# One 4 KB PSUM tile for both halves of a score group, and value products over two query tiles

## The chip, the cores and the metric

The kernel runs on one NeuronCore of a Trainium2 chip. Its engines are TensorE (PE in the profile, with its weight loads as PEld), VectorE (DVE), ScalarE (ACT), GpSimd (POOL) and SyncE (SP), which issues the DMAs. The metric is the device time of one execution in microseconds. Three runs of the kernel before took 1154.95, 1155.72 and 1156.66 us; the median is 1155.72 us.

## The reference

Two layers of a transformer work on 256 context and 256 latent tokens of width 1024. A layer modulates its input, projects it, and has three groups of attention heads side by side: A, six heads of differential attention (two softmax maps of 32-wide queries and keys per head, the second taken off the first with a learned weight); B, six heads with a neighbourhood window and a bias; C, four heads with compressed queries and keys, 96 wide. Then come an output projection, a norm, a gated ConvFFN and a norm. Context tokens read context alone, latent tokens read both; the second layer computes latent queries only.

```python
def _diff_attend(q, k, v, lam, scale):
    s = jnp.einsum('bhqcd,bhkcd->bhcqk', q, k).astype(jnp.float32) * scale
    p = jax.nn.softmax(s, axis=-1)
    p = p[:, :, 0] - lam * p[:, :, 1]
    return jnp.einsum('bhqk,bhkd->bhqd', p.astype(v.dtype), v)

def _softmax_attend(q, k, v, scale):
    s = jnp.einsum('bhqd,bhkd->bhqk', q, k).astype(jnp.float32) * scale
    p = jax.nn.softmax(s, axis=-1)
    return jnp.einsum('bhqk,bhkd->bhqd', p.astype(v.dtype), v)
```

## The kernel before

Weights are split into a high and a low part (`whi` by ACT at L121, `wlo` by DVE at L122), and each product is three matmuls (`mm3`, L134 to L136). The projections for heads A, B and C and the attention units that use them are traced in an order given by the string `ORDERS` (one unit is two heads); a scheduler then sets each engine's own order from that trace, and every engine works through its order strictly.

An attention unit goes over the streams "lat" (512 keys) and, in the first layer, "ctx" (256 keys), and in each over two query tiles of 128 rows. For each query tile `sco` makes **a score group**: two score maps, one per PSUM bank (`sc`, two tiles of 512 floats). For A these are the two maps of one head, for B the two heads of the unit; both have three matmuls per map (`score3`, L626), and the two maps lie in different row groups of the PE array (32 rows each for A, 64 for B). C has one matmul per head (L831). So there are 24 + 12 lat groups and 12 + 6 ctx groups of A and B, and 12 pairs of C.

`softmax_rows` does, for each map, a row maximum (DVE, L381), the exponential with its row sum (ACT, L384) and a reciprocal (DVE, L385). A then multiplies the second reciprocal with the learned weight (L701), scales the second map (L702) and joins the two (L703); B and C scale each map (L674), and B first adds its bias to the map in PSUM (L745). The probabilities are transposed on PE (L392) and copied by ACT (L393) into `pT`, and the value products (`pv`, L400) run once per query tile with 128 columns for each of the two heads, which lie in the two column halves of the array. `drain` keeps transposes and value products one step behind the scores.

PSUM has three banks `acc`, one `ada`, two `sc` and two `tp`. The `sc` banks also serve early projections (`evb`), a value projection (`proj_vk`) and, between the layers, `early`.

Of the kernel before, what the change touches and what calls it, by code (L numbers as in the profile page):

```python
# [77 lines left out]
def build(nc, tc, st, I, out):  # L78
# [18 lines left out]
    def acc():  # L97
        return bank("acc", 3)
# [2 lines left out]
        return bank("ada", 1)  # L101

    def scp():
        return bank("sc", 2)

    def tpp():
        return bank("tp", 2)
# [277 lines left out]
        V.reciprocal(sums[:, 1:2], sums[:, 0:1])  # L385
        return p, sums

    def to_pT(ap, p, nk):
        pT = ap.tile([P, 4, 128], F32, tag="pT", name="pT", bufs=4)
        pt = tpp()  # L390
        for kc in range(nk // P):
            T.transpose(pt[:, 128 * kc:128 * kc + 128], p[:, 128 * kc:128 * kc + 128], ident)  # L392
        S.copy(pT[:, 0:nk // P, :], pt[:, 0:nk].rearrange("p (k q) -> p k q", q=P))  # L393
        return pT

    def pv(po, qt, pTs, vt, c0, nk):
        n = nk // P
        for kc in range(n):
            for e in range(2):
                T.matmul(po[64 * e:64 * e + 64, 128 * qt:128 * qt + 128],  # L400
                         lhsT=vt[:, kc, c0 + 64 * e:c0 + 64 * e + 64],
                         rhs=pTs[e][:, kc, :], start=(kc == 0), stop=(kc == n - 1), tile_position=(0, 64 * e))

# [86 lines left out]
    nxt = load_round(1)  # L490
    ada_round(0, raws)
    ef = [acc() for _ in EF]
    evb = {pr: scp() for pr in (1, 0)}
    for s in range(4):
        ks = (2 * s, 2 * s + 1)
        w = split_early(wes[s])
# [39 lines left out]
    for l in range(L):  # L536
# [60 lines left out]

        def proj_vk():
            w = vkw
            for t in (2, 3, 0, 1):  # L600
                tok = slice(128 * t, 128 * t + 128)
                po = acc() if last and t % 2 else scp()
                for k in range(KD):
                    hi, lo = w[k // 3 * 3]
                    mm3(po[:, 0:288], hT["hi"][:, k, tok], hT["lo"][:, k, tok], hi[:, k % 3, :], lo[:, k % 3, :],
                        k == 0, k == KD - 1)
                pump(PF)
                S.copy(vt[:, t, 256:544], po[:, 0:288])
# [31 lines left out]

        def heads(i, sco, vv, c0, fin):
            for name, q0, nk in streams:
                box = {}
                for qt in range(2):
                    qs = slice(q0 - q0c + 128 * qt, q0 - q0c + 128 * qt + 128)
                    pTs = []

                    def finish(qt=qt, pTs=pTs, box=box, nk=nk, q0=q0):
                        if qt == 0:
                            box["po"] = tpp()  # L650
                        pv(box["po"], qt, pTs, vv, c0 + 128 * i, nk)
                        if qt == 1:
                            fin(box["po"][:, 0:256], slice(q0 - q0c, q0 - q0c + 256))

                    for e in range(2):
                        p = sco(2 * i + e, e, qs, qt, nk, name)

                        def transposed(p=p, e=e, pTs=pTs, nk=nk, finish=finish):
                            pTs.append(to_pT(ap, p, nk))
                            if e == 1:  # L660
                                late[1].append(finish)

                        late[0].append(transposed)
                        drain(0, 1)
                        drain(1, 1)
# [29 lines left out]

        def attn_a(i):
            def sco(h, e, qs, qt, nk, name):
                banks = [scp() for _ in range(2)]
                score3(banks, aqs[i], aks[i], 32, 64 * e, qs, nk)
                (p0, s0), (p1, s1) = [softmax_rows(sc, nk, ap, f"p{m}") for m, sc in enumerate(banks)]  # L700
                V.tensor_tensor(s1[:, 1:2], s1[:, 1:2], lam[:, 2:3], ALU.mult)  # L701
                V.tensor_scalar_mul(p1[:, 0:nk], p1[:, 0:nk], s1[:, 1:2])  # L702
                V.scalar_tensor_tensor(p0[:, 0:nk], p0[:, 0:nk], s0[:, 1:2], p1[:, 0:nk], ALU.mult, ALU.add)  # L703
                return p0

            def fin(po, c):
                sq = ap.tile([P, 256], F32, tag="sq", name="sq", bufs=2)
                S.activation(sq, po, AF.Square)
                pm = tpp()
                T.matmul(pm[:, 0:256], lhsT=K["bones"], rhs=sq, start=True, stop=True)  # L710
# [19 lines left out]
        def attn_b(i):  # L730
            banks = []

            def sco(h, e, qs, qt, nk, name):
                if e == 0:
                    banks[:] = [scp() for _ in range(2)]
# [12 lines left out]
            heads(i, sco, vt, 416 if i else 384, simple_fin(3 + i))  # L748
# [77 lines left out]
                S.copy(mq[h // 2][64:96, h % 2, :], q[32 * h:32 * h + 32, qc])  # L826

        def attn_c(i):
            def sco(h, e, qs, qt, nk, name):
                sc = scp()  # L830
                T.matmul(sc[:, 0:nk], lhsT=mq[i][0:96, e, qs], rhs=mk[i][0:96, e, 0:nk], start=True, stop=True)  # L831
                return normed(sc, nk)

            heads(i, sco, vm, 0, simple_fin(6 + i))

# [10 lines left out]
                not done and kk == 0, len(done) == 3 and kk == 1)  # L846

        def out_early(jb):
            for hf in range(2 if last else 1):
                w = wsplit(I["w_out"][l, hf, jb], 1024)  # L850
                for t in toks:
# [305 lines left out]
        def tail2(ts):  # L1157
# [5 lines left out]
            if 2 in ts:  # L1163
                flush()
                new_h()
            else:
                for i in (12, 13, 14):
                    w = kview(wsplit(I["w_f"][l + 1, i], 1024), KD)
                    early[i] = (acc() if i < 14 else scp(), w, [(CTX, LO + HI)] if i == 14 else [])
                    f_mm(early[i][0], w, 0, LO + HI, LAT, True, i < 14)  # L1170
                w = {kb: kview(wsplit(I["w_v"][l + 1, 0, kb], 1024), 4) for kb in range(2)}
                early["v"] = ({1: scp(), 0: acc()}, w, LO + HI, (0,))
# [107 lines left out]
```

## Time and profile before

| | us |
|---|---|
| median of three runs | 1155.72 |
| profiled execution | 1158.58 |
| its span | 1156.5 |
| PE busy | 1107.0 (96%) |
| DVE busy | 836.1 (72%) |
| ACT busy | 591.2 (51%) |

The span holds the instructions; about 2 us lie around it. Matmuls are pipelined, so the time that one takes is the distance to the start of the next, not its own duration. Attention lies at 118 to 309 us in the first layer and at 785 to 927 us in the second; between and behind them PE works through the FFN without a gap.

### The profile page before, as it was taken

To read this page: it belongs to the slowest core of one execution; us is meant where nothing else is said; L and a number is where in the kernel's file an instruction comes from. 1 tells how busy PE (TensorE), PEld (TensorE's weight loads), DVE (VectorE), ACT (ScalarE), POOL (GpSimd) and SP (SyncE) were. 2 spreads that over 40 slices of the span, in tenths; PEclk is the share of its full clock that TensorE was granted. 3 is DMA by queue.
4 is the path that set the end of the run, shared out by engine and by line. 5 is a ranking of instruction groups with operands and counts; after the bars stand their busy time and mean duration, and the time that the engine had idled before them with its cause. 6 is when DMAs were issued, how large, how long until landed. Compare 5 with 4: busy or idle time off the path is not lost.

```text
span 1156.5 us, 17907 instructions
## 1 busy us (share of the span) xinstructions
PE 1107.0 (96%) x6776; PEld 902.1 (78%) x6776; DVE 836.1 (72%) x1505; ACT 591.2 (51%) x1063; POOL 83.8 (7%) x104
## 2 busy tenths in 40 slices
PE   5999999999998999999999999999999979999997
PEld 3877666686778888887888877897778758999985
DVE  4544677757588887986977687666766777888755
ACT  4345556656548644444352245555555656666541
POOL 0000100003123000000000002110000420000000
PEclk9999999999999999999999999998999988999999
DMA  9767112112143554643558894533111333555662
GB/s 362 295 241 279 58 37 74 37 37 86 51 164 97 197 169 144 199 152 116 186 174 309 311 328 131 176 94 99 53 55 56 128 132 121 183 183 188 201 203 89
DMA packets 58213, 179.19 MB, mean 155 GB/s; under 512 B 7024, under 2 KB 12432, under 8 KB 58128
## 3 DMA queue, kind: packets, MB, share of 16 engines
q1 hardware_dynamic: 58128, 178.05, 45.8%
q8 instruction: 54, 0.88, 0.3%
q14 instruction: 31, 0.25, 0.1%
HBM read 176.94 MB, written 1.08 MB: 154 GB/s over the span
## 4 chain that ended last, share of the span: by engine, by line
PE 85%; DVE 6%; ACT 2%; issue 2%; POOL 2%; DMA 2%; SPq 0%; DVEq 0%; POOLq 0%; ACTq 0%
PE acc L134 21%; PE acc L135 21%; PE acc L136 21%; PE sc L626 6%; PE tp L392 3%; PE tp L400 3%; PE sc L831 2%; DVE wlo L122 1%; PE sc L134 1%; PE sc L135 1%; PE sc L136 1%; POOL xn L344 1%; DMA rawr<-in_w_ada_e 1%; PE ada L234 1%; PE ada L136 1%
## 5 line engine op out<-in xcount | busy, mean ns | idle before, releaser
L121 ACT CAST whi<-raw 128x1024 fp32r<-128x1024 f32 (+3 forms) x204 | 212.0, 1043 | 248.7 <-PE acc L135 124.4
L122 DVE TENSOR_TENSOR wlo<-raw,whi 128x1024 fp32r<-128x1024 f32 (+3 forms) x204 | 248.4, 1221 | 121.4 <-ACT whi L121 117.1
L134 PE MATMUL acc<-hhi,whi 128*128 128x256 f32 (+1 forms) x960 | 327.3, 341 | 3.5 <-ACT hhi L360 3.5
L135 PE MATMUL acc<-hlo,whi 128*128 128x256 f32 (+1 forms) x960 | 325.4, 339 | 0.5 <-DVE hlo L361 0.3
L136 PE MATMUL acc<-hhi,wlo 128*128 128x256 f32 (+1 forms) x960 | 324.1, 338 | 0.4 <-DVE wlo L122 0.4
L134 PEld LDWEIGHTS acc<-hhi,whi 128*128 128x128 f32 x960 | 184.7, 193 | 28.2 <-issue 5.4
L135 PEld LDWEIGHTS acc<-hlo,whi 128*128 128x128 f32 x960 | 184.9, 193 | 22.2 <-issue 3.6
L136 PEld LDWEIGHTS acc<-hhi,wlo 128*128 128x128 f32 x960 | 184.6, 192 | 22.1 <-issue 3.8
L384 ACT ACTIVATE p<-sc,nm 128x512 f32<-128x512 f32 (+1 forms) x132 | 81.4, 619 | 26.0 <-DVE nm L381 24.5
L381 DVE TENSOR_REDUCE nm<-sc 128x1 f32<-128x512 f32 (+1 forms) x132 | 77.3, 598 | 22.7 <-PE sc L626 15.9
L393 ACT COPY pT<-tp 128x512 f32<-128x512 f32 (+1 forms) x96 | 49.4, 516 | 56.2 <-PE tp L392 55.8
L626 PE MATMUL sc<-stk,stq 32*128 32x512 f32 (+3 forms) x324 | 75.0, 392 | 1.0 <-ACT p L384 0.9
L626 PEld LDWEIGHTS sc<-stk,stq 32*128 32x128 f32 (+1 forms) x324 | 41.6, 183 | 26.4 <-issue 11.5
L1064 ACT ACTIVATE u<-acc,conv 128x256 f32<-128x256 f32 (+1 forms) x94 | 60.8, 647 | 1.4 <-PE acc L136 1.3
L1067 DVE SCALAR_TENSOR_TENSOR u<-acc,conv,u 128x255 f32<-128x255 f32 (+1 forms) x94 | 55.1, 586 | 6.3 <-ACT u L1064 6.3
L1068 DVE SCALAR_TENSOR_TENSOR u<-acc,conv,u 128x255 f32<-128x255 f32 (+1 forms) x94 | 55.4, 589 | 2.3
L215 DVE SCALAR_TENSOR_TENSOR ac<-raw,scT,ac 128x1024 f32<-128x1024 f32 x42 | 53.4, 1281 | 4.7 <-DMA raw<-in_w_ada 4.6
L392 PE MATMUL tp<-ident,p 128*128 128x128 f32 x320 | 52.6, 279 | 0.6 <-DVE p L674 0.5
L392 PEld LDWEIGHTS tp<-ident,p 128*128 128x128 f32 x320 | 36.8, 140 | 20.8 <-issue 8.5
L134 PE MATMUL acc<-whi,gBhi 128*128 128x512 f32 x133 | 52.0, 392 | 0.0
L135 PE MATMUL acc<-wlo,gBhi 128*128 128x512 f32 x133 | 51.9, 390 | 0.0
L136 PE MATMUL acc<-whi,gBlo 128*128 128x512 f32 x133 | 51.8, 391 | 0.0
(282 smaller groups left out, 1816.6 us busy)
## 6 DMA issues: line engine op xcount, KB each, us to landing
raw<-in_w_up SPq DMA_DIRECT2D x94, 512.0 KB
raw<-in_w_down SPq DMA_DIRECT2D x53, 512.0 KB
adalo<-in_w_ada SPq DMA_DIRECT2D x32, 512.0 KB
raw<-in_w_f SPq DMA_DIRECT2D x27, 512.0 KB
rawr<-in_w_ada SPq DMA_DIRECT2D x24, 512.0 KB
raw<-in_w_ada SPq DMA_DIRECT2D x24, 512.0 KB
raw<-in_w_out SPq DMA_DIRECT2D x16, 512.0 KB
rawr<-in_w_ada_e SPq DMA_DIRECT2D x12, 512.0 KB
```

What stands on the lines that cost most here:

```text
L121: S.copy(hi, raw)
L122: V.tensor_tensor(lo, raw, hi.bitcast(F32), ALU.subtract)
L134: T.matmul(o, lhsT=lh, rhs=rh, start=first, stop=False)
L135: T.matmul(o, lhsT=lh, rhs=rl, start=False, stop=False)
L136: return T.matmul(o, lhsT=ll, rhs=rh, start=False, stop=last).ins
L381: V.reduce_max(nm, sc[:, 0:nk], axis=AX.X, negate=True)
L384: hT["exp"] = S.activation(p[:, 0:nk], sc[:, 0:nk], AF.Exp, bias=nm, accum_out=sums[:, 0:1]).ins
L392: T.transpose(pt[:, 128 * kc:128 * kc + 128], p[:, 128 * kc:128 * kc + 128], ident)
L626: T.matmul(sc[:, 0:nk], lhsT=q[r, a, qs], rhs=k[r, b, 0:nk], start=t == 0, stop=t == 2, tile_position=(r.start, 0))
L1064: S.activation(t, po[:, c], AF.Identity, scale=cw[:, 1:2], bias=cw[:, 3:4])
L1067: V.scalar_tensor_tensor(t3[:, :, 1:], p3[:, :, 0:255], cw[:, 0:1], t3[:, :, 1:], ALU.mult, ALU.add)
L1068: V.scalar_tensor_tensor(t3[:, :, 0:255], p3[:, :, 1:], cw[:, 2:3], t3[:, :, 0:255], ALU.mult, ALU.add)
```

## The change

`sc` becomes one tile of 1024 floats with one buffer, so two banks are taken and released together. `attn_c` issues both heads' scores at once. `pT` holds two query tiles, and `pv` runs once per unit and stream, with 256 columns. `proj_vk`, `evb` and the early projections between the layers take both halves of one tile. `out_early` first drains the value products.

```diff
     def scp():
-        return bank("sc", 2)
+        t = ps.tile([P, 1024], F32, tag="sc", name="sc", bufs=1)
+        return [t[:, 0:512], t[:, 512:1024]]
...
-    def to_pT(ap, p, nk):
-        pT = ap.tile([P, 4, 128], F32, tag="pT", name="pT", bufs=4)
+    def to_pT(p, nk, pT, qt):
...
-        S.copy(pT[:, 0:nk // P, :], pt[:, 0:nk].rearrange("p (k q) -> p k q", q=P))
-        return pT
+        S.copy(pT[:, 0:nk // P, 128 * qt:128 * qt + 128], pt[:, 0:nk].rearrange("p (k q) -> p k q", q=P))
...
-                T.matmul(po[64 * e:64 * e + 64, 128 * qt:128 * qt + 128],
+                T.matmul(po[64 * e:64 * e + 64, 0:256],
...
-                po = acc() if last and t % 2 else scp()
+                if not pos:
+                    pos = scp()
+                po = acc() if last and t % 2 else pos.pop(0)
...
-                box = {}
+                pTs = [ap.tile([P, 4, 256], F32, tag="pT", name="pT", bufs=4) for _ in range(2)]
+
+                def finish(pTs=pTs, nk=nk, q0=q0):
+                    po = tpp()
+                    pv(po, pTs, vv, c0 + 128 * i, nk)
+                    fin(po[:, 0:256], slice(q0 - q0c, q0 - q0c + 256))
...
-                            pTs.append(to_pT(ap, p, nk))
-                            if e == 1:
+                            to_pT(p, nk, pTs[e], qt)
+                            if e == 1 and qt == 1:
                                 late[1].append(finish)
...
         def attn_c(i):
+            banks = []
+
             def sco(h, e, qs, qt, nk, name):
-                sc = scp()
-                T.matmul(sc[:, 0:nk], lhsT=mq[i][0:96, e, qs], rhs=mk[i][0:96, e, 0:nk], start=True, stop=True)
-                return normed(sc, nk)
+                if e == 0:
+                    banks[:] = scp()
+                    for n, sc in enumerate(banks):
+                        T.matmul(sc[:, 0:nk], lhsT=mq[i][0:96, n, qs], rhs=mk[i][0:96, n, 0:nk], start=True, stop=True)
+                return normed(banks[e], nk)
...
         def out_early(jb):
+            drain(1, 0)
```

The scheduler's order changes with it. On PE, in the second A unit of the first layer, before the change (`sc` are scores, `acc` a projection, `tp` with `ident` a transpose of probabilities):

```order
L626 MATMUL sc<-stk,stq 128x512 x3
L135 MATMUL acc<-hlo,whi 128x512
L392 MATMUL tp<-ident,p 128x128 x4
L626 MATMUL sc<-stk,stq 128x512 x3
L136 MATMUL acc<-hhi,wlo 128x512
L134 MATMUL acc<-hhi,whi 128x512
L135 MATMUL acc<-hlo,whi 128x512
L626 MATMUL sc<-stk,stq 128x512 x3
L136 MATMUL acc<-hhi,wlo 128x512
L392 MATMUL tp<-ident,p 128x128 x4
L626 MATMUL sc<-stk,stq 128x512 x3
```

On PE in the last A unit of the first layer and at the start of the first B unit behind it, after the change (`tp` with `pT,vt` is a value product; L135 to L137 are here the lines of `mm3`, L628 is the scores' and L399 the value product's):

```order
L628 MATMUL sc<-stk,stq 128x512 x6
L392 MATMUL tp<-ident,p 128x128 x4
L628 MATMUL sc<-stk,stq 128x512 x6
L392 MATMUL tp<-ident,p 128x128 x4
L628 MATMUL sc<-stk,stq 128x256 x6
L392 MATMUL tp<-ident,p 128x128 x4
L399 MATMUL tp<-pT,vt 64x256 x4
L628 MATMUL sc<-stk,stq 128x256 x4
L710 MATMUL tp<-sq,bones 128x256
L628 MATMUL sc<-stk,stq 128x256 x2
```

The score groups no longer come in halves of three with projections between them, but as six (49 of the 54 groups of A and B; five have one or a few other matmuls within). In this last stretch of the layer hardly a projection is left between them.

On DVE, in an A unit of the first layer before the change (`nm` is the negated row maximum, `sums` the row sum of which L385 takes the reciprocal; the numbers tell the tiles apart):

```order
L385 RECIPROCAL sums_1783<-sums_1783 128x1
L381 TENSOR_REDUCE nm_1810<-sc_1802 128x1
L385 RECIPROCAL sums_1789<-sums_1789 128x1
L701 TENSOR_TENSOR sums_1789<-sums_1789,lam_665 128x1
L702 TENSOR_SCALAR p_1788<-p_1788,sums_1789 128x512
L381 TENSOR_REDUCE nm_1816<-sc_1803 128x1
L703 SCALAR_TENSOR_TENSOR p_1782<-p_1782,sums_1783,p_1788 128x512
L385 RECIPROCAL sums_1813<-sums_1813 128x1
```

And on DVE in an A unit after the change (L382 is the maximum's line, L386 the reciprocal's; tile `sums_1949` belongs to the first map of the group `sc_1939`, `sums_1955` to the second):

```order
L382 TENSOR_REDUCE nm_1946<-sc_1939 128x1
L386 RECIPROCAL sums_1949<-sums_1949 128x1
L382 TENSOR_REDUCE nm_1952<-sc_1939 128x1
L386 RECIPROCAL sums_1955<-sums_1955 128x1
L701 TENSOR_TENSOR sums_1955<-sums_1955,lam_664 128x1
L702 TENSOR_SCALAR p_1954<-p_1954,sums_1955 128x512
L703 SCALAR_TENSOR_TENSOR p_1948<-p_1948,sums_1949,p_1954 128x512
L382 TENSOR_REDUCE nm_1990<-sc_1983 128x1
```

Before, maxima of the next group (`sc_1802`, `sc_1803`) stood among the reciprocals and scalings of the one ahead of it; now all of a group's DVE work mostly stands in one piece, and the reciprocal of the first map stands ahead of the maximum of the second.

## Rows read from the trace of the kernel before

**Rows 1.** The page: busy time of an engine; a line's busy time, mean ns.

```profile
PE 1107.0 (96%) x6776; PEld 902.1 (78%) x6776; DVE 836.1 (72%) x1505; ACT 591.2 (51%) x1063; POOL 83.8 (7%) x104
...
L122 DVE TENSOR_TENSOR wlo<-raw,whi 128x1024 fp32r<-128x1024 f32 (+3 forms) x204 | 248.4, 1221 | 121.4 <-ACT whi L121 117.1
```

**Rows 2.** Stretches of attention: length, busy us of each engine, clock, DMA share.

```profile
118.00:159.30 41.30, 40.97 (x236) 28.30 (x232) 26.78 (x70) 21.73 (x57) 3.25 (x4) 1.00 0.17 52
159.30:261.70 102.40, 102.40 (x611) 73.53 (x610) 75.28 (x204) 61.58 (x159) 0.00 (x0) 1.00 0.14 47
261.70:309.00 47.30, 46.07 (x326) 32.24 (x324) 36.10 (x87) 28.71 (x77) 14.48 (x18) 1.00 0.26 81
785.00:825.00 40.00, 39.75 (x207) 30.43 (x207) 24.47 (x55) 20.83 (x44) 2.63 (x3) 0.91 0.25 80
825.00:895.40 70.40, 70.08 (x461) 54.62 (x460) 48.46 (x109) 38.97 (x86) 0.00 (x0) 1.00 0.16 55
895.40:927.00 31.60, 31.54 (x219) 22.74 (x219) 24.93 (x47) 19.54 (x39) 13.33 (x16) 1.00 0.41 132
```

**Rows 3.** PE in order of time, split score groups: start, duration, what.

```profile
196.39 0.40 PE L134 MATMUL acc<-hhi,whi 128*128 128x512 f32 x1
196.72 0.96 PE L626 MATMUL sc<-stk,stq 32*128 32x512 f32 x3
197.61 0.50 PE L135 MATMUL acc<-hlo,whi 128*128 128x512 f32 x1
...
203.98 0.62 PE L626 MATMUL sc<-stk,stq 32*128 32x256 f32 x3
```

**Rows 4.** PE in order of time: whole score groups and value products.

```profile
209.43 1.09 PE L400 MATMUL tp<-pT,vt 128*64 128x128 f32 x16
210.46 0.80 PE L626 MATMUL sc<-stk,stq 32*128 32x256 f32 x6
211.19 1.09 PE L400 MATMUL tp<-pT,vt 128*64 128x128 f32 x16
...
219.92 0.96 PE L626 MATMUL sc<-stk,stq 32*128 32x512 f32 x6
```

**Rows 5.** PE in order of time: 256-column products in four column groups.

```profile
109.44 1.50 PE L234 MATMUL ada<-rawr,scT 128*32 128x256 f32 x24
110.87 0.50 PE L134 MATMUL acc<-hhi,whi 128*128 128x512 f32 x1
```

**Rows 6.** All engines in order of time, a lat softmax of A.

```profile
222.62 1.28 DVE L381 TENSOR_REDUCE nm<-sc 128x1 f32<-128x512 f32 x2
...
223.34 0.69 ACT L384 ACTIVATE p<-sc,nm 128x512 f32<-128x512 f32 x1 [0.55 <-DVE nm L381]
...
224.02 0.68 ACT L384 ACTIVATE p<-sc,nm 128x512 f32<-128x512 f32 x1
...
224.33 1.03 PEld L626 LDWEIGHTS sc<-stk,stq 32*128 32x128 f32 x6 [0.35 <-ACT p L384]
...
224.82 0.16 DVE L385 RECIPROCAL sums<-sums 128x1 f32<-128x1 f32 x1 [0.51 <-ACT p L384]
```

**Rows 7.** All engines in order of time: DVE's maximum behind its scores, scalings.

```profile
197.72 0.69 DVE L381 TENSOR_REDUCE nm<-sc 128x1 f32<-128x512 f32 x1 [0.21 <-PE sc L626]
...
198.71 0.49 DVE L702 TENSOR_SCALAR p<-p,sums 128x512 f32<-128x512 f32 x1
...
200.08 0.74 DVE L703 SCALAR_TENSOR_TENSOR p<-p,sums 128x512 f32<-128x512 f32 x1
```

**Rows 8.** All engines in order of time: softmax at 256 columns, and B's bias.

```profile
276.48 0.76 DVE L381 TENSOR_REDUCE nm<-sc 128x1 f32<-128x256 f32 x2 [0.20 <-PE sc L626]
...
277.14 0.48 ACT L384 ACTIVATE p<-sc,nm 128x256 f32<-128x256 f32 x1
...
277.74 0.16 DVE L385 RECIPROCAL sums<-sums 128x1 f32<-128x1 f32 x1 [0.51 <-ACT p L384]
...
279.62 0.76 DVE L745 TENSOR_TENSOR sc<-sc,rpb 128x256 f32<-128x256 f32 x2 [0.46 <-issue]
```

More of the change, by code (lines that the diff above doesn't have):

```diff
@@ L392, in to_pT, with pv @@
             T.transpose(pt[:, 128 * kc:128 * kc + 128], p[:, 128 * kc:128 * kc + 128], ident)
-        S.copy(pT[:, 0:nk // P, :], pt[:, 0:nk].rearrange("p (k q) -> p k q", q=P))
-        return pT
-    def pv(po, qt, pTs, vt, c0, nk):
+        S.copy(pT[:, 0:nk // P, 128 * qt:128 * qt + 128], pt[:, 0:nk].rearrange("p (k q) -> p k q", q=P))
+    def pv(po, pTs, vt, c0, nk):
         n = nk // P
@@ L492, in build @@
     ef = [acc() for _ in EF]
-    evb = {pr: scp() for pr in (1, 0)}
+    evb = dict(zip((1, 0), scp()))
     for s in range(4):
@@ L599, in proj_vk @@
             w = vkw
+            pos = []
             for t in (2, 3, 0, 1):
                 tok = slice(128 * t, 128 * t + 128)
-                po = acc() if last and t % 2 else scp()
+                if not pos:
+                    pos = scp()
+                po = acc() if last and t % 2 else pos.pop(0)
                 for k in range(KD):
@@ L642, in heads, with transposed @@
             for name, q0, nk in streams:
-                box = {}
+                pTs = [ap.tile([P, 4, 256], F32, tag="pT", name="pT", bufs=4) for _ in range(2)]
[3 more added lines that the diff above has]
+                    fin(po[:, 0:256], slice(q0 - q0c, q0 - q0c + 256))
                 for qt in range(2):
                     qs = slice(q0 - q0c + 128 * qt, q0 - q0c + 128 * qt + 128)
[L646 to L653, printed above, removed]
                     for e in range(2):
                         p = sco(2 * i + e, e, qs, qt, nk, name)
-                        def transposed(p=p, e=e, pTs=pTs, nk=nk, finish=finish):
-                            pTs.append(to_pT(ap, p, nk))
-                            if e == 1:
+                        def transposed(p=p, e=e, qt=qt, pTs=pTs, nk=nk, finish=finish):
+                            to_pT(p, nk, pTs[e], qt)
+                            if e == 1 and qt == 1:
                                 late[1].append(finish)
@@ L697, in sco @@
             def sco(h, e, qs, qt, nk, name):
-                banks = [scp() for _ in range(2)]
+                banks = scp()
                 score3(banks, aqs[i], aks[i], 32, 64 * e, qs, nk)
@@ L734, in sco @@
                 if e == 0:
-                    banks[:] = [scp() for _ in range(2)]
+                    banks[:] = scp()
                     score3(banks, bqs[i], bks[i], 64, 0, qs, nk)
@@ L828, in attn_c @@
         def attn_c(i):
+            banks = []
             def sco(h, e, qs, qt, nk, name):
-                sc = scp()
-                T.matmul(sc[:, 0:nk], lhsT=mq[i][0:96, e, qs], rhs=mk[i][0:96, e, 0:nk], start=True, stop=True)
-                return normed(sc, nk)
+                if e == 0:
+                    banks[:] = scp()
+                    for n, sc in enumerate(banks):
+                        T.matmul(sc[:, 0:nk], lhsT=mq[i][0:96, n, qs], rhs=mk[i][0:96, n, 0:nk], start=True, stop=True)
+                return normed(banks[e], nk)
             heads(i, sco, vm, 0, simple_fin(6 + i))
@@ L1166, in tail2 @@
             else:
+                e14, ev = scp()
                 for i in (12, 13, 14):
                     w = kview(wsplit(I["w_f"][l + 1, i], 1024), KD)
-                    early[i] = (acc() if i < 14 else scp(), w, [(CTX, LO + HI)] if i == 14 else [])
+                    early[i] = (acc() if i < 14 else e14, w, [(CTX, LO + HI)] if i == 14 else [])
                     f_mm(early[i][0], w, 0, LO + HI, LAT, True, i < 14)
                 w = {kb: kview(wsplit(I["w_v"][l + 1, 0, kb], 1024), 4) for kb in range(2)}
-                early["v"] = ({1: scp(), 0: acc()}, w, LO + HI, (0,))
+                early["v"] = ({1: ev, 0: acc()}, w, LO + HI, (0,))
                 for e in range(2):
```

## The prediction

> **What bounds the kernel now.** I read the page first: PE is busy 96% of the span [rows 1]. Then the stretches that hold attention [rows 2]: in the first layer PE has no idle time at 159.3 to 261.7 us (A) and next to none at 261.7 to 309 (B); the same holds in the second layer from 825 to 927. DVE is the second engine, 75.3 us of the 102.4 in the first layer's A, at full clock throughout. Everything outside these stretches is untouched work, so the question is what these take: 41.3 us (C), 102.4 (A), 47.3 (B) in layer one, 40.0 (C), 70.4 (A), 31.6 (B) in layer two. They are full of PE work, but that work is made long: a look at PE in order of time shows half a score group of 512 columns, three matmuls, holding PE 0.89 us (196.72 to 197.61) [rows 3], while all six, issued as alternating pairs, show the same 0.96 us of duration as those three [rows 3, 4]. Two row groups of the array work at once when their matmuls stand next to each other; a split group pays twice.
>
> **What PE saves.** In the order before, 31 runs of three lat matmuls stand alone, about 15 groups: 15 x 0.89 = 13.4 us. Of ctx there are 23 such runs, 11 groups: a half lasts 0.62 in its row and a whole 0.80 (0.73 to the next start), so about 2 x 0.55 - 0.73 = 0.4 each, 4 us [rows 3, 4]. About eight lat groups do stand whole but with the three of one map ahead of the three of the other, and miss about 0.5 us each: 4 us. Each run also costs about 0.1 us at its edge (196.39 to 196.72 is 0.33 for a matmul that otherwise takes 0.23), and there are 32 runs fewer: 3 us.
>
> Value products: 16 records, eight products of 128 columns, take 1.03 us (209.43 to 210.46) [rows 4]; the two column halves run together, so that is four pairs of 0.22 and about 0.15 of edge. At 256 columns the nearest rows are the modulation's, 24 records in groups of four, each group at once, in 1.43 us: 0.22 us for a 256-column record, twice that for a product of two records [rows 5]. Eight wide products are then four pairs of 0.43 and one edge, 1.88 us, against 2.06 for two calls before: 0.18 x 16 lat calls and about half that x 8 ctx, 4 us. If the weight loads set the pace instead, it would be up to 1 us a call, 20 in all; the 0.22 of the rows are the columns' pace, so I take 4. In all PE's work shrinks by some 29 us, which is the gain if PE stays the bound.
>
> **What the single tile does to the chain.** This is the part I trust most. The order on DVE after the change is, for each group of A: maximum 1, reciprocal 1, maximum 2, reciprocal 2, the three scalings, maximum 1 of the next. Reciprocal 1 waits for exponential 1, and DVE takes its work strictly in order: maximum 2 now stands behind the whole of exponential 1, and the next group's scores wait for exponential 2, since both banks come free together. Before, the first bank came free after its own exponential, and the next group's maxima stood between the scalings. I count a group's period from exponential 2 to exponential 2, in us from its start.
>
> Lat group of A: reciprocal 2 at 0.80 (224.02 to 224.82), the small multiplication at 1.0, scaling 1.2 to 1.7 (0.49), joining to 2.4 (0.74); the scores are issued at 0.99 (223.34 to 224.33) and read 1.0 later (196.72 to 197.72), 2.0, so DVE is the later one. Maximum 1 at 2.4, exponential 1 at 3.12 (0.72, from 222.62 to 223.34), reciprocal 1 at 3.92, maximum 2 at 4.08, exponential 2 at 4.80 [rows 3, 6, 7]. The period is 4.8 us with no other work in it. Ctx: reciprocal after 0.60 (277.14 to 277.74), maximum 0.38 (half of 0.76), scalings two thirds of the above: 3.4 us [rows 8]. Lat group of B: two bias additions of 0.38 each, one ahead of each maximum, one scaling ahead of maximum 2: 0.99 + 1.0 + 0.38 + 0.72 + 0.80 + 0.16 + 0.38 + 0.49 + 0.72 = 5.6 us; ctx of B: about 3.1 [rows 6 to 8].
>
> Between these chains PE does projections. From the order after, at 0.23 us for a 512-column and 0.12 for a 256-column matmul, PE has 4.4 to 5.9 us to do per lat group and 3.3 to 4.7 per ctx group for the first two and a half A units of layer one. So work and chain are about level there, and the chain sets the pace where a weight split (1.2 us, row L122) stands in it [rows 1]. For the last 17 groups of the layer the order leaves only some 42 us of PE work, and there the chain alone decides.
>
> **The sum, by stretches.** Layer one, A: 12 x 4.8 + 12 x 3.4 = 98.4 us. DVE's 75.3 us hold about 56 of softmax (24 maxima of 0.6 and so on), so 19 of splits and projections; while it waits for an exponential about 0.9 us of such work fits in twice per lat group, half that per ctx group. I take 7 of the 19 as not fitting (bounds 0 and 19), and 2 for groups in which PE has more to do than the chain: 107 against 102.4 us, +5. B: 6 x 5.6 + 5 x 3.1 = 49 against 47, +2. C: the pair issued together makes max, exponential, reciprocal serial too, but PE has 5 to 6 us to do per lat pair: 40 against 41, -1. Layer two: A 12 x 4.8 = 58 plus 6 unhidden = 64 against 70.4, -6; B has five steps of 5.6 = 28, plus 7 for two steps in which the order leaves 7 and 10 us of PE work = 35 against 31.6, +4. In layer two projections were the ballast that kept PE long, so the shorter scores show; in layer one they don't.
>
> Beside that: PE has less to do behind the last scores of each layer (-2); `proj_vk` and the early products take and release two banks at once (+1, one copy's wait each, between 0 and 3); ACT's weight casts now stand in the same chain as the exponentials (+1, between 0 and 8: there are about 20 of 1 us in attention). The sum is +4 us on the profiled 1158.6, or 1162.6; that run was 1158.58 where the median is 1155.72, a ratio of 0.9975: **1160 us**. The three sums that could move it are the unhidden work (-13 to +25 over both layers), ACT's casts, and what the two periods really are: 0.3 us on 36 lat groups is 11 us.
>
> The Trainium skill has a rule against this change: "Perfetto Trace Analysis", Optimizing Tensor Performance, says that independent groups of matmuls should rotate through PSUM banks so that ACT's and DVE's evacuation of one lies beside the matmuls of the next. The rows agree as far as they go: with two tiles the scores at 224.33 start while the second exponential of the group ahead still runs [rows 6]. By the rule alone the change loses; what the rows add is that PE wins up to 29 us back.
>
> **Rivals.**
> *PE stays the bound (chance 0.24).* If maximum 2 is not held up by exponential 1 as long as I read (say 4.0 us a lat group, 2.9 a ctx group, 4.6 and 2.6 in B), then wherever PE has 4.4 us to do per group the full saving shows, and only the end of layer one waits: 2 x 4.0 + 4 x 2.9 + 6 x 4.6 + 5 x 2.6 = 60 us against 42 of PE work, 18 lost. 29 - 18 = 11: 1147.6, or 1145; with the wait at the end smaller too, down to 1127. For it: PE is the only engine that is full, and the order of before also has reciprocals between maxima. Against it: DVE's strict order.
> *The serial chain also takes in the weight splits (0.18), the slower side.* Place: DVE between the two maxima of a group. About 24 splits of 1.2 us stand there in the new order; if ACT's part of each (the cast of 1.0 us) comes late, the split waits for it with maximum 2 behind it, and nothing is hidden: 24 x 0.5 us more than in my sum, 12 us, so 1174.6 or 1172. It decides once a lat group takes more than about 5.2 us on the mean. For it: splits do wait for casts (117 us in all, row L122) [rows 1]. Against: the casts stand early in ACT's order.
> That the change doesn't do what it says is out: 49 of the 54 groups of A and B stand whole in the order.
>
> **How the numbers follow.** My forecast, chain-bound attention with about no net change, has 0.58, with a range of its own from 1150 to 1168. Faster or slower by 0.2% (2.3 us) is about what a measurement of this kernel tells from no change, so "same" is 1153.4 to 1158.0. Of the forecast's 0.58 I put 0.09 below it, 0.14 in it and 0.35 above; the first rival is faster throughout, the second slower. Faster 0.33, same 0.14, slower 0.53. The range reaches down to 1141, into the first rival, and up to 1174, leaving out some 0.1 on either side.
>
> **What the profile after would show.** Right: L626's successor in runs of six with total PE time near 45 us instead of 75; PE idle for the first time in the first layer's attention, at its end above all, with ACT's exponential as the releaser; second maxima that start 0.9 us or more behind the start of exponential 1; layer one's attention longer, layer two's shorter. Wrong: lat groups of A that follow each other in under 4.4 us (then the first rival), or DVE waiting for `whi` between two maxima in most groups (the second). The value products' place is right if their calls of 16 records last about 1.9 us, and wrong if about 1.1.

## The result, and the profile after

The changed kernel takes 1197.01 us (median of 4 runs, 1196.09 to 1200.06) against 1155.66 for the kernel before in the same comparison: a ratio of 1.0362, with a 95% interval from 1.0341 to 1.0383. It is 41 us slower. Forecast were 1160 us, with a range that ended at 1174: the direction was right, the size wrong by a factor of ten (+4 us on the profiled execution were forecast).

In the changed kernel most lines stand one or two lower: scores L628, maximum L382, exponential L385, reciprocal L386, value products L399. These are lines of its page (busy time, mean, and idle time just before with what ended it; in the slices of `PEclk` a 9 is full clock).

```profile
PE 1100.7 (92%) x6456; PEld 881.0 (74%) x6456; DVE 836.2 (70%) x1505; ACT 590.7 (49%) x1063; POOL 84.5 (7%) x104
...
PEclk9999999976689999999999999999999997999999
...
L386 DVE RECIPROCAL sums<-sums 128x1 f32<-128x1 f32 x132 | 21.4, 162 | 86.4 <-ACT p L385 85.9
L628 PE MATMUL sc<-stk,stq 32*128 32x512 f32 (+3 forms) x324 | 53.4, 431 | 17.4 <-ACT p L385 17.3
```

The last two lines as they read for the kernel before:

```profile
L385 DVE RECIPROCAL sums<-sums 128x1 f32<-128x1 f32 x132 | 20.9, 159 | 19.2 <-ACT p L384 18.8
L626 PE MATMUL sc<-stk,stq 32*128 32x512 f32 (+3 forms) x324 | 75.0, 392 | 1.0 <-ACT p L384 0.9
```

PE is busy 92% instead of 96% [rows 1]. The scores do cost it less, 53.4 us instead of 75.0, but it now waits for exponentials, and so does DVE: ahead of the reciprocals it waits 85.9 us (18.8 before). In four slices in a row, 239 to 359 us, the clock is down to 6 to 8 tenths, and in one much later to 7.

The stretches of attention, in the order of [rows 2] (layer one C, A, B, then layer two): length, busy us of each engine, clock, DMA share.

```profile
119.10:158.30 39.20, 39.20 (x195) 27.85 (x191) 27.24 (x74) 22.55 (x58) 2.25 (x2) 1.00 0.18 55
158.30:274.50 116.20, 101.82 (x572) 70.47 (x571) 76.99 (x196) 61.11 (x158) 0.00 (x0) 0.92 0.16 55
274.50:346.90 72.40, 52.36 (x237) 30.42 (x237) 33.67 (x90) 28.48 (x78) 13.55 (x18) 0.66 0.06 17
822.30:859.00 36.70, 36.56 (x184) 28.24 (x185) 24.21 (x58) 21.11 (x42) 2.63 (x3) 0.95 0.28 86
859.00:925.30 66.30, 63.73 (x405) 47.00 (x404) 47.25 (x102) 37.38 (x84) 0.00 (x0) 1.00 0.18 58
925.30:967.20 41.90, 36.48 (x196) 23.72 (x197) 29.18 (x56) 22.55 (x46) 14.35 (x18) 0.96 0.34 104
```

Against [rows 2] that is -2.1, +13.8, +25.1, -3.3, -4.1 and +10.3 us, 39.7 together; the span grew by 39.4. So the whole loss lies in attention, 25 us of it in layer one's B, where PE is busy for 52 of 72 us and at a granted clock of 0.66. That is a mean: at any time the clock is at one of its two levels, 1.00 (2.4 GHz) or 0.50 (1.2 GHz).

One lat group of A, all engines in order of time (start, duration, what), from its scores to the next group's:

```profile
196.19 0.99 PE L628 MATMUL sc<-stk,stq 32*128 32x512 f32 x6
...
197.22 0.69 DVE L382 TENSOR_REDUCE nm<-sc 128x1 f32<-128x512 f32 x1
...
198.06 0.69 ACT L385 ACTIVATE p<-sc,nm 128x512 f32<-128x512 f32 x1
...
198.88 0.16 DVE L386 RECIPROCAL sums<-sums 128x1 f32<-128x1 f32 x1 [0.96 <-ACT p L385]
198.96 0.67 DVE L382 TENSOR_REDUCE nm<-sc 128x1 f32<-128x512 f32 x1
...
199.96 0.68 ACT L385 ACTIVATE p<-sc,nm 128x512 f32<-128x512 f32 x1
...
201.13 0.96 PE L628 MATMUL sc<-stk,stq 32*128 32x512 f32 x6
```

Maximum, exponential, maximum, exponential, one at a time. Before, the second maximum ran while the first exponential did [rows 6]. Counted over all 132 exponentials in order of time, 61 ran beside a maximum before, 22.9 us in all; after the change none does.

And one lat group of B, where the loss per group is largest in layer one (7.2 us from scores to scores on the mean, 4.8 before):

```profile
283.03 1.53 PE L628 MATMUL sc<-stk,stq 64*128 64x512 f32 x6 [0.46 <-ACT p L385]
...
284.67 0.43 DVE L745 TENSOR_TENSOR sc<-sc,rpb 128x256 f32<-128x256 f32 x1 [0.64 <-PE sc L628]
...
285.13 0.69 DVE L382 TENSOR_REDUCE nm<-sc 128x1 f32<-128x512 f32 x1
...
286.12 0.69 ACT L385 ACTIVATE p<-sc,nm 128x512 f32<-128x512 f32 x1
...
287.02 0.43 DVE L745 TENSOR_TENSOR sc<-sc,rpb 128x256 f32<-128x256 f32 x1
...
287.33 0.72 POOL L743 TENSOR_TENSOR rpb<-rpb,m 128x256 f32<-128x256 f32 x1 [4.85 <-DMA rpb<-in_rpb]
287.36 0.98 DVE L674 TENSOR_SCALAR p<-p,sums 128x512 f32<-128x512 f32 x1
...
288.26 0.68 DVE L382 TENSOR_REDUCE nm<-sc 128x1 f32<-128x512 f32 x1
...
289.15 0.58 ACT L393 COPY pT<-tp 128x512 f32<-128x512 f32 x1 [2.25 <-PE tp L392]
...
289.63 0.69 ACT L385 ACTIVATE p<-sc,nm 128x512 f32<-128x512 f32 x1
...
290.47 1.01 PE L628 MATMUL sc<-stk,stq 64*128 64x256 f32 x6 [1.35 <-ACT p L385]
```

From scores to scores 7.44 us, where 5.6 were forecast. That the second bias addition waits for the first exponential was in the forecast. Not in it were three things: the scores take 1.53 us at the lower clock, where 1.0 was taken; the scaling takes 0.98 us, where 0.49 was; and the second exponential, whose maximum is done at 288.94, stands behind the copy of the first map's transposes on ACT until 289.63.

### The profile page after: what moved, and what is told of

Read it like the earlier page. It is cut to its first block, busy times and chain, and to the rows that moved or that the text cites. A ratio compares the mean times of both kernels' runs of the same rounds, so it can differ in the third digit from the quotient of the medians.

```text
span 1195.9 us, 17229 instructions
## 1 busy us (share of the span) xinstructions
PE 1100.7 (92%) x6456; PEld 881.0 (74%) x6456; DVE 836.2 (70%) x1505; ACT 590.7 (49%) x1063; POOL 84.5 (7%) x104
## 4 chain that ended last, share of the span: by engine, by line
PE 77%; DVE 10%; ACT 6%; issue 3%; POOL 2%; DMA 1%; SPq 0%; DVEq 0%; ACTq 0%; POOLq 0%
PE acc L135 19%; PE acc L136 19%; PE acc L137 19%; PE tp L392 4%; PE tp L399 4%; PE sc L628 3%; ACT p L385 2%; DVE wlo L123 2%; PE sc L835 2%; PE sc L135 1%; ACT pT L393 1%; PE ada L235 1%; PE sc L136 1%; PE sc L137 1%; ACT whi L122 1%
## 5 line engine op out<-in xcount | busy, mean ns | idle before, releaser
L135 PE MATMUL acc<-hhi,whi 128*128 128x256 f32 (+1 forms) x960 | 322.2, 336 | 4.0 <-ACT hhi L361 4.0
L137 PE MATMUL acc<-hhi,wlo 128*128 128x256 f32 (+1 forms) x960 | 321.8, 336 | 0.0
L135 PEld LDWEIGHTS acc<-hhi,whi 128*128 128x128 f32 x960 | 183.2, 191 | 24.2 <-ACT hhi L361 4.7
L137 PEld LDWEIGHTS acc<-hhi,wlo 128*128 128x128 f32 x960 | 183.2, 191 | 20.0 <-issue 3.0
L385 ACT ACTIVATE p<-sc,nm 128x512 f32<-128x512 f32 (+1 forms) x132 | 81.6, 619 | 45.6 <-DVE nm L382 45.2
L393 ACT COPY pT<-tp 128x512 f32<-128x512 f32 (+1 forms) x96 | 49.2, 513 | 89.4 <-PE tp L392 89.2
L382 DVE TENSOR_REDUCE nm<-sc 128x1 f32<-128x512 f32 (+1 forms) x132 | 78.1, 591 | 15.6 <-PE sc L835 9.1
L392 PE MATMUL tp<-ident,p 128*128 128x128 f32 x320 | 60.4, 309 | 26.1 <-DVE p L674 17.0
L386 DVE RECIPROCAL sums<-sums 128x1 f32<-128x1 f32 x132 | 21.4, 162 | 86.4 <-ACT p L385 85.9
L628 PE MATMUL sc<-stk,stq 32*128 32x512 f32 (+3 forms) x324 | 53.4, 431 | 17.4 <-ACT p L385 17.3
L628 PEld LDWEIGHTS sc<-stk,stq 32*128 32x128 f32 (+1 forms) x324 | 28.8, 210 | 38.2 <-ACT p L385 29.9
L135 PE MATMUL acc<-whi,gBhi 128*128 128x512 f32 x133 | 52.0, 392 | 0.0
```

The lines of the kernel that those rows point to most:

```text
L135: T.matmul(o, lhsT=lh, rhs=rh, start=first, stop=False)
L137: return T.matmul(o, lhsT=ll, rhs=rh, start=False, stop=last).ins
L382: V.reduce_max(nm, sc[:, 0:nk], axis=AX.X, negate=True)
L385: hT["exp"] = S.activation(p[:, 0:nk], sc[:, 0:nk], AF.Exp, bias=nm, accum_out=sums[:, 0:1]).ins
L393: S.copy(pT[:, 0:nk // P, 128 * qt:128 * qt + 128], pt[:, 0:nk].rearrange("p (k q) -> p k q", q=P))
L628: T.matmul(sc[:, 0:nk], lhsT=q[r, a, qs], rhs=k[r, b, 0:nk], start=t == 0, stop=t == 2, tile_position=(r.start, 0))
```

## The experiments

The theory: the joined tile makes a group's maxima and exponentials serial, and idle PE then loses its clock. The rivals: the value products with 256 columns; the release of both banks together; projections used up too early. Times are medians, each with its ratio to the kernel before in its own comparison. "A1" is the time from the first exponential of layer one's A to that of its B, "B1" from there to the last exponential of that layer, "A2" and "B2" the same in layer two, all from the profiled execution; "scores" is the busy time of the three-matmul scores, "clock" the granted one at 280 to 320 us.

| kernel | us | ratio, 95% | A1 | B1 | A2 | B2 | scores | clock |
|---|---|---|---|---|---|---|---|---|
| before | 1155.7 | | 102.1 | 45.7 | 69.6 | 34.7 | 75.0 | 1.00 |
| changed | 1197.0 | 1.0362 (1.0341 to 1.0383) | 117.4 | 71.4 | 67.5 | 42.8 | 53.4 | 0.67 |
| 1 two tiles, wide products | 1160.5 | 1.0042 (1.0026 to 1.0059) | 103.3 | 46.0 | 69.9 | 38.9 | 81.4 | 1.00 |
| 2 joined tile, narrow products | 1194.9 | 1.0341 (1.0319 to 1.0362) | 117.3 | 67.6 | 69.7 | 39.3 | 50.7 | 0.67 |
| 3 changed, maxima first | 1180.4 | 1.0225 (1.0205 to 1.0245) | 105.0 | 64.6 | 65.7 | 43.7 | 53.6 | 0.67 |
| 4 two tiles, narrow products | 1155.9 | 1.0011 (1.0001 to 1.0021) | 102.0 | 47.6 | 69.6 | 34.7 | 75.0 | 1.00 |
| 5 changed, matmuls added freely | 1204.0 | 1.0420 (1.0398 to 1.0441) | 116.0 | 69.0 | 71.8 | 44.0 | 51.7 | 0.67 |
| 6 as 3, units spread | 1179.1 | 1.0213 (1.0195 to 1.0231) | mixed | mixed | 65.7 | 41.2 | 52.9 | 0.70 |
| 7 as 1, second bank first | 1159.2 | 1.0034 (1.0021 to 1.0047) | 101.3 | 51.5 | 69.1 | 36.6 | 76.6 | 1.00 |
| 8 as 4, scores chained | 1156.9 | 1.0012 (1.0001 to 1.0023) | 101.8 | 50.7 | 68.8 | 32.8 | 68.6 | 1.00 |
| 9 changed, matmuls added at the transposes | 1188.8 | 1.0293 (1.0273 to 1.0312) | 118.9 | 58.4 | 68.3 | 41.2 | 49.2 | 1.00 |
| 10 = 3 and 9 | 1169.3 | 1.0118 (1.0094 to 1.0142) | 104.2 | 55.4 | 65.1 | 39.5 | 49.4 | 0.96 |
| 11 as 1, scores chained | 1154.9 | 0.9997 (0.9988 to 1.0005) | 98.9 | 52.2 | 68.0 | 35.8 | 68.9 | 0.96 |
| 12 before, scores chained | 1155.5 | 1.0008 (0.9998 to 1.0018) | 101.6 | 48.1 | 68.6 | 33.8 | 70.0 | 1.00 |

### Which half of the change: 1 and 2

Experiment 1 edits the changed kernel by

```diff
-        t = ps.tile([P, 1024], F32, tag="sc", name="sc", bufs=1)
-        return [t[:, 0:512], t[:, 512:1024]]
+        return [bank("sc", 2) for _ in range(2)]
```

> The changed kernel, but the scores go into two tiles of one bank, as before the change; the wide value products, the paired C scores and the early drain stay. If the joined tile makes the loss (softmax of the second map serial behind the first, whole groups behind both exponentials), this lands near the kernel before: 1148 to 1165 us, the B units of layer one some 47 us from first to last group instead of 72, the A stage near 102 us, granted clock 1.00 between 160 and 350 us. If the wide value products (with the transposes and pT that they hold) make it, it stays near the changed kernel: 1185 to 1200 us.

Experiment 2 keeps the joined tile and puts `to_pT`, `pv` and `heads` back as they were, without the early drain.

> The changed kernel with the value products of before (128 columns, one query tile a call, pT per query tile, no early drain); the joined score tile and the paired C scores stay. If the joined tile makes the loss: 1190 to 1205 us. If the wide value products make it: 1150 to 1165 us. If both have a share, between.

Measured 1160.5 and 1194.9: the joined tile is the loss. With two tiles B1 is back at 46.0 us and the clock at 1.00. Experiments 2 and 4 differ in the lines of the tile alone, and lie 39 us apart (1194.9 against 1155.9). The wide value products cost 4.6 us with two tiles (1160.5 against 1155.9 in experiment 4). With the joined one it is 2.1 us (1197.0 against 1194.9), and the two intervals overlap.

### The order on VectorE: 3

```diff
-                (p0, s0), (p1, s1) = [softmax_rows(sc, nk, ap, f"p{m}") for m, sc in enumerate(banks)]
+                nms = [row_max(sc, nk) for sc in banks]
+                (p0, s0), (p1, s1) = [softmax_rows(sc, nk, ap, f"p{m}", nms[m]) for m, sc in enumerate(banks)]
```

and in B and C the same, in B with both bias additions ahead of the maxima.

> The changed kernel with both bias adds and both row maxima of a group issued on VectorE ahead of the first reciprocal; same operations and tiles. If the loss is the serial order on VectorE (second maximum behind the first exponential and its reciprocal, 1.2 to 2 us of each group), about half to two thirds of the 41 us come back: 1168 to 1180 us, A lat groups 4.4 us, B lat groups 5.5 us. If it is the release (a group's scores wait for both exponentials whatever the order), within 8 us of the changed kernel: 1189 to 1200 us.

Measured 1180.4: 17 us of the 41 came back, most of it in A1 (117.4 to 105.0), a little short of what was expected. The groups did not get as short as expected: from scores to scores 5.1 us for A's lat groups and 7.5 for B's (means of layer one), where 4.4 and 5.5 were expected. A lat group of B in time order:

```profile
294.21 0.96 DVE L744 TENSOR_TENSOR sc<-sc,rpb 128x256 f32<-128x256 f32 x2 [0.90 <-PE sc L631]
295.19 0.59 ACT L396 COPY pT<-tp 128x512 f32<-128x512 f32 x1 [1.35 <-PE tp L395]
295.20 1.29 DVE L382 TENSOR_REDUCE nm<-sc 128x1 f32<-128x512 f32 x2
296.52 0.69 ACT L388 ACTIVATE p<-sc,nm 128x512 f32<-128x512 f32 x1 [0.75 <-DVE nm L382]
...
297.20 0.68 ACT L388 ACTIVATE p<-sc,nm 128x512 f32<-128x512 f32 x1
```

Now the first exponential waits for the second maximum (done at 296.49), though it needs only the first (done at 295.89) and ACT has been idle for 0.75 us. In all 54 groups of A and B the first exponential starts only behind the second maximum's end; in some others of them ACT has other work just ahead of it. Again none of the 132 exponentials runs beside a maximum. The order was one share; the mutual waiting of ACT and DVE on one tile stays, whatever the order.

### The release of both banks: 7 and 8

Experiment 7, on 1, was to make a group with two tiles wait for both exponentials: a score of the second bank is issued first, the other five behind it.

> The kernel with two score tiles of one bank and wide value products (1160.5 us), with the second bank's scores issued first and the first bank's behind them, so that a group is issued together and waits for both exponentials of the group before, as with the joined tile, though the tiles are apart. If that release is what is left of the loss once both maxima go first, this lands by the kernel with the maxima first: 1174 to 1186 us, with B of layer one at 58 to 66 us. If the joined tile costs something else (waits that the tile adds), it stays at 1158 to 1166 us.

Measured 1159.2, but the edit didn't do what it was for: the second map's exponential simply went first as well, so the bank issued first was still the one freed first (from 872.03 us on scores start while the second exponential, from 871.88 to 872.55, still runs). Experiment 8 ties both orders down, on the kernel of 4:

```diff
-                for n, sc in enumerate(banks):
+                for n, sc in reversed(list(enumerate(banks))):
...
+                    st.enter_context(tc.issue_after(m.ins))
...
+        with tc.issue_after(hT.get("exp", hT["tab"])):
```

> Two score tiles of one bank and narrow value products (1155.9 us), with the six score matmuls of a group chained in order, so that five of the six wait for both exponentials of the group before: the release of the joined tile, without its joining. The second map's maximum can still run beside the first map's exponential. If that release is what is left of the loss once both maxima go first: 1170 to 1182 us, clock under 0.95 between 280 and 345 us. If the loss needs the joined tile itself, whose maxima and exponentials never run at the same time: 1148 to 1160 us, and with the score matmuls of a group in pairs (busy 53 us instead of 75) this may be the best kernel.

A lat group of A in it:

```profile
870.71 1.28 DVE L381 TENSOR_REDUCE nm<-sc 128x1 f32<-128x512 f32 x2
871.42 0.69 ACT L385 ACTIVATE p<-sc,nm 128x512 f32<-128x512 f32 x1 [1.08 <-DVE nm L381]
...
872.10 0.68 ACT L385 ACTIVATE p<-sc,nm 128x512 f32<-128x512 f32 x1
...
872.25 0.50 PE L631 MATMUL sc<-stk,stq 32*128 32x512 f32 x1
...
873.34 0.96 PE L631 MATMUL sc<-stk,stq 32*128 32x512 f32 x5
```

One matmul slips in early, and five of six wait for both exponentials; over 52 groups of A and B no more than one of six ever starts before the second exponential of the group ahead has ended (before, two or three did in 26 of them). The time is 1156.9 us. So releasing both banks late, with the scores chained, costs 1 us in all against experiment 4 (1155.9), and the intervals overlap. That is a net figure: the scores' busy time fell by 6.4 us beside it (75.0 to 68.6), and B1 is 3.1 us longer (50.7 against 47.6), so the release itself may cost a few us (an estimate follows at experiment 12). What experiment 8 keeps is in the first two rows: the exponential starts at 871.42 inside the pair of maxima (46 of 132 do). The expected fall in the scores' time came only in part (68.6 us, not 53).

### The clock: 5 and 9

Experiment 5 adds six matmuls of 128x512 behind each group's scores in the first two B units, into the idle `ada` bank.

> The changed kernel with six added matmuls of 128x512 (results unused, in a bank that is idle there) behind the scores of each lat and context group of the first two B units of a layer, some 1.2 us of TensorE at the upper clock for each group, put where it has nothing else to do. If the fall of the granted clock to 0.67 to 0.78 is part of the loss in B (scores 1.53 us instead of 1.0, transposes 1.11 instead of 0.63, both on the serial chain), the clock is back near 1.00, the B stage of layer one falls from 71 us (first to last exponential) to 60 to 66 us and the kernel to 1185 to 1192 us. If the low clock only follows from waits that stay, it is the same or slower: 1196 to 1208 us.

Measured 1204.0, and it told little: nothing bound the added matmuls to their place, and the scheduler put all 48 of layer one beside A's last groups (230 to 251 us) and most of layer two's into its A (A2 71.8 instead of 67.5), and the clock at 280 to 320 us stayed at 0.67. Experiment 9 binds them:

```diff
         pt = tpp()
+        for j in range(3 if hT.get("fill") else 0):
+            T.matmul(pt, lhsT=hT["hi"][:, 0, 0:128], rhs=hT["hi"][:, 0, :], start=True, stop=True)
```

> The changed kernel with three added matmuls of 128x512 (results overwritten) ahead of the transposes of each softmaxed map of the B units, in the bank that the transposes then fill, so that they stand where TensorE waits for that map. If the low granted clock is part of the loss in B: clock above 0.9 between 280 and 345 us, B of layer one 60 to 67 us instead of 71, kernel 1184 to 1193 us. If it only follows from the waits: 1195 to 1210 us.

The changed kernel, and then experiment 9, in three equal stretches (PE, PEld, DVE, ACT, POOL busy, clock):

```profile
240.00:280.00 40.00, 27.17 (x125) 16.01 (x123) 23.73 (x64) 16.78 (x46) 0.80 (x2) 0.70 0.06 18
280.00:320.00 40.00, 28.97 (x130) 17.20 (x128) 18.69 (x49) 17.80 (x49) 11.16 (x15) 0.67 0.07 22
320.00:360.00 40.00, 29.23 (x146) 17.80 (x147) 18.54 (x49) 17.55 (x41) 1.60 (x2) 0.78 0.13 47
```

```profile
240.00:280.00 40.00, 29.42 (x130) 17.13 (x128) 22.39 (x61) 17.10 (x48) 0.00 (x0) 0.70 0.06 17
280.00:320.00 40.00, 35.37 (x199) 22.02 (x201) 21.49 (x60) 20.29 (x55) 12.96 (x16) 1.00 0.08 24
320.00:360.00 40.00, 37.88 (x190) 26.37 (x187) 24.44 (x53) 17.42 (x36) 1.73 (x2) 1.00 0.39 130
```

Only where B's added matmuls stand, the clock goes back from 0.67 to 1.00, and B1 falls from 71.4 to 58.4 us, more than expected: work that computes nothing makes the kernel 8 us faster. The low clock is a share of its own. How much of the 13 us is the clock by itself is not shown to the last us, since a few of ACT's copies in B moved behind an exponential in the new order (ACT's order differs in 36 of 1063 places).

### Projections used up, and the shares together: 6 and 10

Experiment 6 reorders layer one's units on the kernel of 3, so that projections are left beside B:

```diff
-"... ak0 aq1 C0 aq2 A0 bk1 ak2 A1 bk2 bq1 A2 bk0 bq0 v2 B2 B0 W3 B1 W0 W1"
+"... ak0 aq1 C0 bk0 bq0 A0 aq2 B0 ak2 A1 bk2 v2 B2 bk1 bq1 A2 W3 B1 W0 W1"
```

> The kernel with the maxima first (1180.4 us), with layer one's units in another order: B0 and B2 stand between the A units, so that projections are left beside them, and A2 and B1 come last. Same work. If the remaining loss is that projections are used up beside the A units and the serial B groups have nothing beside them, A and B together fall from 170 us towards the 150 us that the serial chain asks for, with the clock near 1.00: 1160 to 1172 us. If the B groups are slow by themselves, whatever stands beside them: 1177 to 1184 us.

Measured 1179.1, against 1180.4: nothing gained, the second case. The stretch without projections only moved to A2 and B1, which now come last: at 280 to 320 us PE is busy for 24.1 us of the 40, at a clock of 0.70. That B lay behind the projections is thus not what makes the loss; whether yet another order of the units would gain isn't shown. Experiment 10 puts 3 and 9 together.

> The kernel with both maxima first (1180.4 us) and, for the B units, the added matmuls that stood ahead of the transposes (1188.8 us with them alone, B of layer one 58 us and clock 1.00). If the serial order and the low clock are two shares that add up (17 and 8 us off 1197): 1170 to 1175 us, B of layer one 52 to 57 us. If they are one and the same loss (a shorter chain leaves the added matmuls no room, or the clock no longer falls), 1177 to 1183 us.

Measured 1169.3, just under the range expected of adding shares. The ledger, as differences of medians: order of the maxima 17 us (1197.0 to 1180.4), added matmuls and with them the clock 11 us behind it (to 1169.3; 8 us without it), and 14 us that are left against before, 9.7 of them in B1 (55.4 against 45.7). That most of the rest is the waiting of ACT and DVE on one tile is what experiment 8 points to; it was not taken out by itself while the tile stayed joined, and the late release may have a part in it.

### The value products, and a better kernel: 4, 11 and 12

Experiment 4 has both undone, so that only the paired C scores are left.

> Two score tiles of one bank and the value products of before (128 columns); of the change only the paired C scores and the tiles taken in pairs are left. It splits the 5.6 us that the kernel with two tiles and wide value products still lost against before (1160.5 against 1154.8). If the wide value products make them: 1151 to 1156 us. If the paired C scores and the order of the tiles make them: 1159 to 1162 us.

Measured 1155.9, near the top of the first range: C and the pairs cost nothing that shows. Why the wide products cost 4.6 us was asked by experiment 11, which chains the scores as in 8 on the kernel of 1:

> Two score tiles of one bank, the score matmuls of a group chained in order, and the wide value products. With two tiles and wide value products alone the kernel was at 1160.5 us, with scores busy for 81 us instead of 75. If that rise in the scores (more of them split) is why the wide value products cost 4.5 us, chaining removes it: 1150 to 1156 us, scores at 60 to 70 us. If the wide value products cost by themselves (transposes and pT held longer): 1158 to 1163 us.

Its scores and its value products of A and B (PE, busy us and mean ns), and below them those of 1:

```profile
L629 PE MATMUL sc<-stk,stq 32*128 32x512 f32 (+3 forms) x324 | 68.9, 407 | 1.6 <-ACT p L385 1.5
...
L399 PE MATMUL tp<-pT,vt 128*64 128x256 f32 x240 | 30.8, 395 | 0.0
```

```profile
L627 PE MATMUL sc<-stk,stq 32*128 32x512 f32 (+3 forms) x324 | 81.4, 393 | 0.2
...
L398 PE MATMUL tp<-pT,vt 128*64 128x256 f32 x240 | 30.6, 387 | 0.0
```

1154.9 us: the loss is gone and the products take as long as in 1. So it lay in the order of the scores, more of which stood split beside the wide products (15 of the 54 groups whole in 1, 22 before), and not in the products. Experiment 12 chains the scores in the kernel before.

> The kernel before with one edit: the score matmuls of a group of A and B chained in order, so that they are issued together; tiles, value products and C as before. If scores issued together shorten the stretches in which TensorE is never idle: 1148 to 1153 us, scores below 70 us instead of 75. If a group then waits for its second bank as much as it gains: 1154 to 1158 us.

1155.5, the second case: 5 us less of score time and no gain. In 8, 11 and 12 alike the time came out some 5 to 7 us above what the fall of the scores' busy time alone would give (6.4 us less and 1.0 lost; 12.5 less and 5.6 gained; 5.0 less and nothing gained). So, as an estimate, waiting for both exponentials costs up to that much in these kernels; it was not measured apart. None of the kernels beats the one before; 11 and 12 equal it.

## Why the prediction was wrong

*Right.* Maximum 2 behind exponential 1: so in every group of A and B. PE idle for the first time, at the end of layer one's attention, with the exponential as releaser: 17.3 us ahead of the scores. Layer one's attention longer; layer two's A shorter, by 4.1 us, with 6 forecast. (Layer two's attention as a whole, C, A and B, became 2.9 us longer, where it was to be shorter.) Layer one's C -2.1 against -1. The wide call of 16 records holds PE 1.88 us (197.69 to 199.57), as forecast; at full clock, in experiment 1, the products of A and B take 30.6 us instead of 33.2 and those of C 10.0 instead of 12.8: 5.4 us saved, 4 forecast. The scores fell to 53.4 us, part of it at the lower clock (49.4 in experiment 10, at 0.96), against some 45.

*The step that failed* is the size of the serial chain, and worst "B: 6 x 5.6 + 5 x 3.1 = 49 against 47, +2". Measured were 72.4 us, +25; layer two's B was +10 against +4; layer one's A +14 against +5. The periods, as means of the score starts in layer one: A's lat groups 5.5 us against 4.8 and its ctx groups 4.2 against 3.4, B's lat groups 7.2 against 5.6 and its ctx groups 5.7 against 3.1. Three things were not in them:

1. The sum held only the softmax's own operations. ACT works in order too, and between exponentials it copies transposes. In the B group shown the second exponential starts 0.7 us behind its maximum's end, right after such a copy, whose transposes wait for the first map's scaling. In layer one's six lat groups of B the step from maximum 2 to exponential 2 took 1.77 us on the mean, where the sum has 0.72, and in five of them a copy stands right ahead of that exponential. In B's ctx groups the step from maximum 1 to exponential 1 took 1.19 us instead of some 0.4, behind a copy in all six; in layer one's lat groups of A it took 1.14 instead of 0.72. The step from exponential 1 to maximum 2 in B's lat groups, with the bias addition and the scaling in it, was right: 1.84 against 1.83. The rival that let other work into the chain was given 0.18, with weight splits on DVE as its place. The decisive point it named, 5.2 us per lat group, was passed, but not through splits: 12 of them stand between a group's two maxima in the trace, not 24, and DVE waited 95.0 us for `whi`, less than the 117.1 before.
2. Durations were taken from rows at full clock. The forecast said that the chain alone decides for the last 17 groups of layer one, with 42 us of PE work in them, and didn't ask what becomes of PE's clock there: 0.66, with scores of 1.53 us instead of 1.0, so that B's lat groups took 1.90 us from the scores to maximum 1 where the sum has 1.38. Filling PE's waits was worth 8 to 11 us (experiments 9 and 10). The Trainium skill, "TensorE: Matmul & The Clock Gate", HAM oscillation, tells of a kernel whose waits for DMA between groups of matmuls throttle the clock again and again; here the waits are for the softmax, and the trace agrees, with 0.67 back to 1.00 once matmuls fill them.
3. The tile's effect was taken to be the order on DVE and the late release. Experiment 3 changed the order and got 17 us; experiment 8 shows that the release, with the scores chained, costs 1 us net. The rest of the mechanism was missing: with one tile the program lets ACT and DVE at it only in turns, though they want different banks. In every kernel with the joined tile, in either order of the maxima, none of the 132 exponentials runs beside a maximum; in every one with two tiles 46 or more do.

The Trainium skill's rule that was set against the change ("Perfetto Trace Analysis", Optimizing Tensor Performance: groups rotate through banks, so that one's evacuation lies beside the next one's matmuls) had the right sign. Its reason doesn't carry the size here: in experiment 8 five of six matmuls wait for the whole evacuation, and 1 us net is lost. What was lost beside it is ACT beside DVE within a group, and the clock. "Advanced Engine Details and Errata", Bank Collisions, in the Trainium skill says that these two may use PSUM at once at full rate if they are in different banks; the trace agrees, with exponentials of 0.69 us beside a maximum [rows 6] as without one in the rows of the A group above. So the chip would have allowed it; the waits come from the tile.

*The rivals.* "PE stays the bound" is out: lat groups never came down to 4.0 us, and PE was idle. With it goes the hope behind the 29 us: PE did get that work off its hands in part, and waited instead.

## What to carry to other kernels

Joining buffers into one tile joins their waits as well: look not only at when the tile is released, but at which engines used its parts at the same time before (here 61 of 132 exponentials). When a chain, not an engine, is to set the pace, sum every in-order engine that the chain passes through, with all that stands in its queue, and not the chain's own operations alone. And where the sum leaves TensorE waiting as here (busy for 52 of 72 us), work out a second sum with its work at the lower clock.

## What the runs showed of the hardware

Added matmuls that compute nothing made a stretch shorter by 13 us (71.4 to 58.4), with a granted clock of 1.00 instead of 0.67 and nearly the same order on ACT and DVE.

And in the B group shown, DVE's scaling took 0.98 us, where the same form takes 0.49 [rows 7], while POOL worked on the bias beside it (from 287.33). The 14 traces hold 896 such scalings (`p<-p,sums`, 128x512). The 690 with no POOL instruction beside them took 0.47 to 0.49 us, and so did the 47 beside POOL's multiplication of the bias alone (L743). Of the 159 beside its addition (`mneg`) 114 took over 0.5 us, up to 1.06. So it is the addition that goes with the slow ones; why was not tested, and the kernel before has them too (6 of 9).
